# Copying the strided queries of the dilated attention groups side by side before the scores read them

## The chip, the cores and the metric

The kernel runs on one core of one Trainium2 chip. A core has five engines, each with its own in-order stream of instructions: TensorE (PE in the profile, with its weight loads listed apart as PEld), VectorE (DVE), ScalarE (ACT), GpSimd (POOL) and SyncE (SP), which here issues most DMAs. They meet through semaphores. The metric is the device time of one execution in microseconds (us); the median of the runs counts.

## The reference, cut to what matters

One decoder layer over 4096 positions: an input projection, eight heads of dilated sliding-window attention, four heads of retention, gates and an output projection. The change touches the scores of the dilated attention. Every head evaluates three branches on the same q, k and v:

```python
DILATED_BRANCHES = ((128, 1), (512, 4), (2048, 16))
def dilated_branch(q, k, v, window, dilation):
    steps = window // dilation            # 128 in every branch
    ...
    qb = gather_stride(q)                 # query t, t+d, t+2d, ...
    kb = with_prev(gather_stride(k))      # block before and own block
    vb = with_prev(gather_stride(v))
    s = jnp.einsum('bhrnqd,bhrnkd->bhrnqk', qb, kb) * (Dh ** -0.5)
    ...
    p = jnp.exp(s - m)
```

A block has 128 queries that lie `dilation` positions apart, and 256 keys. With dilation 1 the queries of a block are neighbours; with dilation 4 or 16 they are every fourth or every sixteenth position.

## The kernel before

**Stages.** Phase 1 projects q, k, v and the retention inputs and stores them in DRAM. Phase 2 does the attention and, woven between its steps, the retention and one more projection (the "filler": its matmuls are named V, Rs, Rk, Ro, Rkv, Rt). Phase 3 does the gates and the output projection. Nothing outside phase 2 is touched.

**Data of a head.** The queries of a head come from DRAM as four tiles `qq[h, t, half]`: t is 0 for the rounded-to-fp32r high part and 1 for the low rest, half is 0 for positions 0 to 2047 and 1 for the others (tiles named q_00, q_10, q_01, q_11, the first digit being t). Each tile holds 128 partitions x 2048 elements of four bytes, in the natural order of positions, and is loaded by four DMAs of 256 KB (`load_q`, issued by SP on line 547). Each of the four names has one buffer. The keys `kk[h]` stand already in an order in which a block's keys come in runs of at least eight neighbours.

**Work of a head.** `head_groups` makes 24 groups ("items") a head, gi 0 to 23, each of four blocks:
- gi 0 to 3: branch 0 (dilation 1), positions of half 0
- gi 4 to 11: branch 1 (dilation 4), alternating: one group in half 0, the next in half 1
- gi 12 to 19: branch 2 (dilation 16), each group with two blocks in either half
- gi 20 to 23: branch 0, positions of half 1

**Order.** `attention` writes the order out by hand, in half-steps: half-step t computes the scores of bank t (two blocks, one PSUM bank). An item has two half-steps; a head has 48, phase 2 has 384. In half-step t the program emits:
- `qk_bank` (line 595, PE): four matmuls S, two for each block (high part, low part). The weights, which TensorE loads before a matmul, are the 128 queries; the keys stream past them. Before the change the weights are read straight from `qq` with a step of 1, 4 or 16 elements.
- `t_bank` (line 632, PE): transposes T of the probabilities of bank t-2.
- `pv_group` (line 665, PE), at even t: the products O with the values of the item two before.
- `exp_row` (line 623, ACT) for bank t-1, `row_max` (line 616, DVE) for bank t, and `t_copy`, which moves T to SBUF (on DVE for an item's first bank, line 644, on ACT for its second, line 642).

The score tiles have two buffers: S of bank t may start once the exponentials of bank t-2 are done. So the loop S, row maximum (DVE), exponential (ACT), S runs over two half-steps. The filler's matmuls are put between the half-steps by a fixed cost table that knows nothing of the weights' step; so many half-steps, so much filler.

**Loads around the change.** At gi 0 of a head the eight DMAs of half 1 of this head are put in a list, of which two leave on SP at each half-step, between stores and other loads; SP takes them in order, and one that has to wait holds those behind it. At gi 20 the eight of half 0 of the next head follow. All DMAs of SP share the core's DMA engines.

**GpSimd in phase 2** does the low parts of the filler's inputs (line 405, 833, 836), a decay product (862) and a small power (924), 263 instructions in all.

Of the kernel before, what the change touches and what calls it, by code (L numbers as in the profile page):

```python
# [9 lines left out]
F32R = mybir.dt.float32r  # L10
# [380 lines left out]
DIL = (1, 4, 16)  # L391
# [17 lines left out]
def load_k(nc, pool, dr, h, dma=None):  # L409
    dma = dma or nc.sync.dma_start  # L410
    t = pool.tile([128, S], F32R, tag="kk", name="kk2")
    for i in range(2):
        for part in range(2):
            p0 = i * 64 + part * 32
            dma(t[p0 : p0 + 32, :].bitcast(F32), dr["k"][i, part, h])
    return t
# [63 lines left out]
def load_q(nc, pool, dr, h, i, half, dma=None):  # L480
    dma = dma or nc.sync.dma_start
    t = pool.tile([128, S // 2], F32R, tag=f"q{i}{half}", name=f"q2_{i}{half}")
    for dup in range(2):
        for part in range(2):
            p0 = dup * 64 + part * 32
            dma(t[p0 : p0 + 32, :].bitcast(F32), dr["q"][i, part, h, :, half * 2048 : (half + 1) * 2048])
    return t


def phase2(tc, io, dr, right, ahead, early3, raw, M):  # L490

    nc = tc.nc
    W2, hcp, kka, qp = (ahead[n] for n in ("w2", "hcp", "kka", "qp"))
    with ExitStack() as ctx:
        def pool(name, bufs, **kw):
            return ctx.enter_context(tc.tile_pool(name=name, bufs=bufs, reuse_waits="tile", **kw))
# [8 lines left out]
        osp = pool("p2os", 3)  # L505
        pp = pool("p2p", 3)
        vp = pool("p2v", 6)
        kkb = pool("p2kb", 1)
        psS = pool("p2pS", 2, space=PSUM)
        psT = pool("p2pT", 2, space=PSUM)  # L510
# [26 lines left out]
        def later(n, fn, *args):  # L537

            delayed.setdefault(clock[0] + n, []).append((fn, args))

        def issue_due():
            for fn, args in delayed.pop(clock[0], []):
                fn(*args)
            room = 250
            while pending and room > 0:
                dst, src = pending.pop(0)
                nc.sync.dma_start(dst, src)
                room -= dst.shape[0] * dst.shape[1] // 512
# [7 lines left out]
        qq = ahead["qq"]  # L556
# [14 lines left out]
        def need_v(h, br, g, ahead=2):  # L571

            i = vqueue.index((h, br, g))
            while vpos[0] <= min(i + ahead, len(vqueue) - 1):
                load_v(*vqueue[vpos[0]])
                vpos[0] += 1

        def qk_bank(it, bank):
            it["P", bank] = pp.tile([128, 2, 256], F32, tag="P", name="P2")
            h, br, blocks = it["h"], it["br"], it["blocks"]  # L580
            s = psS.tile([128, 512], F32, tag="S", name="S2")
            kt_ = kk[h]
            d = DIL[br]
            for j in range(2):
                i = 2 * bank + j
                r, n = blocks[i]
                half, off = divmod(n * 128 * d, 2048)
                off += r
                ks = max(n - 1, 0)
                if br == 0:  # L590
                    rhs = kt_[:, 128 * ks : 128 * ks + 256]
                else:
                    rhs = kt_.rearrange("p (m q) -> p m q", q=8 * d)[:, 16 * ks : 16 * ks + 32, 8 * r : 8 * r + 8]
                for t in range(2):
                    nc.tensor.matmul(  # L595
                        s[:, j * 256 : (j + 1) * 256],
                        qq[h, t, half][:, off : off + 127 * d + 1 : d],
                        rhs,
                        start=(j == 0 and t == 0),
                        stop=(j == 1 and t == 1),  # L600
                        skip_group_check=True,
                    )
            it["S", bank] = s
# [16 lines left out]
        def exp_row(it, i):  # L620
            nm, den = stats[it["h"]]
            sv, c0, col = s_view(it, i)
            nc.scalar.activation(  # L623
                it["P", i // 2][:, i % 2, c0:256], sv, AF.Exp, bias=nm[:, col : col + 1], scale=-1.0, accum_out=den[:, col : col + 1]
            )

        def t_bank(it, bank):

            first = 1 if it["blocks"][2 * bank][1] == 0 else 0
            t = psT.tile([128, 512], F32, tag="T", name="T2")  # L630
            for j in range(first, 4):
                nc.tensor.transpose(  # L632
                    t[:, j * 128 : (j + 1) * 128], it["P", bank][:, j // 2, j % 2 * 128 : j % 2 * 128 + 128], ident
                )
            it["T", bank] = t, first
            return 4 - first

        def t_copy(it, bank):
            t, first = it["T", bank]
            pt = it["pt"][:, 4 * bank + first : 4 * bank + 4, :].rearrange("p a b -> p (a b)")  # L640
            if bank:
                nc.scalar.activation(pt, t[:, first * 128 :], AF.Copy)  # L642
            else:
                nc.vector.tensor_copy(pt, t[:, first * 128 :])
# [8 lines left out]
        def pv_group(it):  # L653

            h, br = it["h"], it["br"]
            o = psO.tile([128, 512], F32, tag="O", name="O2")
            ops = [pv_ops(it, bank) for bank in range(2)]
            for x in range(-max(map(len, ops)), 0):
                for bank in range(2):
                    if -x > len(ops[bank]):  # L660
                        continue
                    r, n, a, m, c0 = ops[bank][x]
                    idx = r * NB_OF[br] + n
                    need_v(h, br, idx // 8)
                    nc.tensor.matmul(  # L665
                        o[64 * bank : 64 * bank + 64, c0 : c0 + 128 * m],
                        vt[h, br, idx // 8][:, idx % 8, :],
                        it["pt"][:, a : a + m, :].rearrange("p a b -> p (a b)"),
                        start=-x == len(ops[bank]),
                        stop=x == -1,  # L670
                        skip_group_check=True,
                    )
            it["O"] = o
# [63 lines left out]
        for h in range(H):  # L737
            for gi, (br, blocks) in enumerate(groups):
                it = dict(h=h, br=br, blocks=blocks, gi=gi)
# [3 lines left out]
        def pv_cost(it):  # L743
            return 190 + 218 * (4 if it["blocks"][2][1] else 3)

        def attention():


            nh = 2 * len(items)

            def half(t):
                return (items[t // 2], t % 2) if 0 <= t < nh else (None, 0)

            for t in range(nh + 12):
                cost = 0
                clock[0] = t
                issue_due()
                it, b = half(t)
                i1, b1 = half(t - 1)
                i2, b2 = half(t - 2)  # L760
                g = (t - 4) // 2 if t % 2 == 0 else -1
                gp = (t - 5) // 2 if t % 2 else -1
                if it and b == 0:
                    h, gi = it["h"], it["gi"]
                    if gi == 0:
                        stats[h] = (
                            sp.tile([128, 96], F32, tag="nm", name="nm2"),
                            sp.tile([128, 96], F32, tag="den", name="den2"),
                        )
                    if h + 1 < H:  # L770
                        if gi == 6:
                            kk[h + 1] = load_k(nc, kkb if h % 2 == 0 else kka, dr, h + 1, soon)
                        if gi == len(groups) - 4:
                            for i in range(2):
                                qq[h + 1, i, 0] = load_q(nc, qp, dr, h + 1, i, 0, soon)
                    if gi == 0:
                        for i in range(2):
                            qq[h, i, 1] = load_q(nc, qp, dr, h, i, 1, soon)
                if it:
                    qk_bank(it, b)  # L780
                    cost += 436
                if i2:
                    cost += t_bank(i2, b2) * TRN
                if 0 <= g < len(items):
                    pv_group(items[g])
                    cost += pv_cost(items[g])
                if 0 <= gp < len(items):
                    o_copy(items[gp])
                if i1:
                    exp_row(i1, 2 * b1)  # L790
                    exp_row(i1, 2 * b1 + 1)
                if i2 and b2:
                    t_copy(i2, b2)
                if it:
                    row_max(it, 2 * b)
                    row_max(it, 2 * b + 1)
                if i2 and not b2:
                    t_copy(i2, b2)
                if i1 and b1 == 1 and i1["gi"] == len(groups) - 1:
                    later(2, end_head, i1["h"])  # L800
                    cost += 2 * TRN
                yield cost
# [197 lines left out]
        n = 2 * len(items)  # L1000
# [360 lines left out]
```

## Time and profile before

| | us |
|---|---|
| median of 3 runs | 2518.52 (2517.79 to 2518.9) |
| the profiled execution: its own time | 2520.2 |
| the profiled execution: span of its trace | 2518.4 |
| of it phase 1, about | 783 |
| of it phase 2, about | 974 |
| of it phase 3, about | 761 |

The granted TensorE clock was 0.984 over the span. In the profile, a row of the windows view gives a stretch, its length, and the busy time of each engine in it with the number of instructions in brackets; a row of the timeline gives start, length, engine, source line, operation, the tile written and the tiles read, and in square brackets how long the engine had been idle and what ended that. A busy time is a union of intervals: TensorE's matmuls overlap their successors a little, since they are pipelined.

### The profile page before, as it was taken

How to read it: one execution, taken by the hardware profiler on the slowest of the kernel's cores; microseconds unless marked ns; L12 is line 12 of the kernel's file. 1: busy time of each engine (PE TensorE's matmuls, PEld its weight loads, DVE VectorE, ACT ScalarE, POOL GpSimd, SP SyncE). 2: the span in 40 equal slices, each digit the busy share in tenths (PEclk: the TensorE clock that was granted, in tenths of full speed). 3: DMA queues.
4: the chain of work that ended last, by engine and by line, in shares of the span. 5: the costliest groups of instructions: out<-in, count | busy, mean ns of one | idle time of the engine just before them, and what ended most of it. 6: DMA issues, size and time to landing. Idle time of an engine off the chain costs nothing.

```text
span 2518.4 us, 41352 instructions
## 1 busy us (share of the span) xinstructions
PE 2434.4 (97%) x14568; PEld 2085.2 (83%) x14568; DVE 1402.4 (56%) x3729; ACT 995.3 (40%) x2868; POOL 558.2 (22%) x569
## 2 busy tenths in 40 slices
PE   7999999999995999999999999998899999999998
PEld 5788888888884888888888888886789899999997
DVE  5544353354252566656666666765756556565564
ACT  4312212222123565656566656666323223232231
POOL 5312112112102222222222222223421212112110
PEclk9999999999997999999999999999899999999999
DMA  5343334334357474738374747545677565665663
GB/s 184 127 145 130 117 128 149 109 134 137 110 154 197 115 177 108 185 93 192 99 183 106 174 120 157 135 114 156 186 157 153 156 149 159 158 154 159 146 154 91
DMA packets 404063, 362.55 MB, mean 144 GB/s; under 512 B 191784, under 2 KB 334760, under 8 KB 398736
## 3 DMA queue, kind: packets, MB, share of 16 engines
q1 hardware_dynamic: 389216, 332.91, 50.6%
q10 hardware_dynamic: 14112, 25.43, 3.2%
q8 instruction: 115, 1.88, 0.3%
q0 software_dynamic: 528, 1.58, 0.2%
q14 instruction: 92, 0.75, 0.1%
HBM read 241.18 MB, written 118.64 MB: 143 GB/s over the span
## 4 chain that ended last, share of the span: by engine, by line
PE 85%; DMA 6%; DVE 3%; issue 1%; ACT 1%; POOL 1%; SPq 1%; ACTq 0%; POOLq 0%; DVEq 0%
PE S L595 12%; PE mm L49 8%; PE mm L50 8%; PE mm L51 8%; PE O L665 7%; PE T L632 6%; PE po L50 4%; PE po L51 4%; PE po L49 4%; PE g L50 4%; PE g L49 4%; PE g L51 4%; PE V L49 3%; PE V L51 2%; PE V L50 2%; DMA wb<-dr_w 1%
## 5 line engine op out<-in xcount | busy, mean ns | idle before, releaser
L616 DVE CUSTOM_DVE_ANT_0 S<-S,mask 128x256 f32<-128x256 f32 (+1 forms) x768 | 309.2, 403 | 345.5 <-PE S L595 251.0
L595 PE MATMUL S<-kk,q 128*128 128x256 f32 x1536 | 369.2, 363 | 35.3 <-DMA q<-dr_q 28.8
L595 PEld LDWEIGHTS S<-kk,q 128*128 128x128 f32 x1536 | 326.4, 274 | 68.8 <-issue 50.6
L623 ACT ACTIVATE P<-S,nm 128x256 f32<-128x256 f32 (+1 forms) x768 | 337.0, 449 | 41.8 <-DVE nm L616 21.1
L51 PE MATMUL g<-h,wg 128*128 128x256 f32 x1024 | 291.1, 284 | 0.0
L632 PE MATMUL T<-ident,P 128*128 128x128 f32 x1368 | 212.8, 273 | 0.5 <-ACT P L623 0.5
L50 PE MATMUL po<-wo,m 128*128 128x512 f32 x512 | 201.7, 394 | 0.0
L51 PEld LDWEIGHTS g<-h,wg 128*128 128x128 f32 x1024 | 198.0, 193 | 0.1
L665 PE MATMUL O<-pt,v 128*64 128x128 f32 (+1 forms) x1968 | 195.4, 324 | 0.2 <-ACT pt L642 0.2
L405 POOL TENSOR_TENSOR hc<-hr,hc 128x512 fp32r<-128x512 f32 x64 | 83.1, 1299 | 488.9 <-ACT hc L404 317.7
L49 PE MATMUL po<-wohi,m 128*128 128x512 f32 x448 | 175.3, 391 | 1.2 <-DVE x L1147 1.2
L51 PE MATMUL po<-wohi,m 128*128 128x512 f32 x448 | 176.4, 394 | 0.0
L665 PEld LDWEIGHTS O<-pt,v 128*64 128x64 f32 x1968 | 121.0, 136 | 60.4 <-issue 31.9
L632 PEld LDWEIGHTS T<-ident,P 128*128 128x128 f32 x1368 | 158.7, 141 | 1.1 <-ACT P L623 1.1
L623 ACT ACTIVATION_READ_ACCUMULATOR P<-S,nm 128x1 f32 x768 | 158.0, 206 | 0.0
L49 PE MATMUL g<-h,wg1hi 128*128 128x256 f32 x512 | 146.3, 287 | 12.0 <-ACT h L439 12.0
L41 ACT ACTIVATE m<-e 128x256 fp32r<-128x256 f32 x128 | 53.3, 417 | 256.1 <-DVE e L1100 147.1
L50 PE MATMUL g<-h,wg1hi 128*128 128x256 f32 x512 | 148.5, 290 | 2.3 <-DVE h L440 1.7
L49 PE MATMUL g<-h,wg0hi 128*128 128x256 f32 x512 | 145.5, 284 | 4.6 <-ACT e L1093 4.6
L159 POOL TENSOR_TENSOR sq<-sq,sq 128x512 f32<-128x512 f32 x56 | 76.2, 1362 | 331.4 <-ACT sq L155 331.4
L50 PE MATMUL g<-h,wg0hi 128*128 128x256 f32 x512 | 145.3, 284 | 0.0
L1154 POOL TENSOR_TENSOR rs<-v,mhalf 128x1 f32<-128x1 f32 x32 | 17.4, 544 | 555.2 <-DVE v L1152 555.2
(201 smaller groups left out, 5675.9 us busy)
## 6 DMA issues: line engine op xcount, KB each, us to landing
hr<-in_xT_dram SPq DMA_DIRECT2D x64, 512.0 KB
q<-dr_q SPq DMA_DIRECT2D x128, 256.0 KB
wb<-dr_w SPq DMA_DIRECT2D x128, 192.0 KB
o<-dr_o SPq DMA_DIRECT2D x192, 128.0 KB
v<-dr_v SPq DMA_DIRECT2D x94, 256.0 KB
xt<-in_xT_dram SPq DMA_DIRECT2D x64, 256.0 KB
dr_q<-hl SPq DMA_DIRECT2D x32, 512.0 KB
dr_k<-hl SPq DMA_DIRECT2D x32, 512.0 KB
```

Source lines behind the costliest of these rows:

```text
L41: nc.scalar.activation(dst[:, 0], src, AF.Copy)
L49: nc.tensor.matmul(out, wh, xh, start=first and i == 0, stop=False)
L50: nc.tensor.matmul(out, wh, xl, start=False, stop=False)
L51: nc.tensor.matmul(out, wl, xh, start=False, stop=last and i == n - 1)
L159: nc.gpsimd.tensor_tensor(sums[b], sums[b], sq, ALU.add)
L405: nc.gpsimd.tensor_tensor(hc[:, :, 1, :], src, hc[:, :, 0, :].bitcast(F32), ALU.subtract)
L595: nc.tensor.matmul(s[:, j * 256 : (j + 1) * 256], qq[h, t, half][:, off : off + 127 * d + 1 : d], rhs, start=(j == 0 and t == 0), stop=(j ...
L616: nc.vector.tensor_tensor_reduce(sv, sv, mask[:, it["br"], c0:256], 1.0, BIG, ALU.add, ALU.min, accum_out=nm[:, col : col + 1])
L623: nc.scalar.activation(it["P", i // 2][:, i % 2, c0:256], sv, AF.Exp, bias=nm[:, col : col + 1], scale=-1.0, accum_out=den[:, col : col + 1])
L632: nc.tensor.transpose(t[:, j * 128 : (j + 1) * 128], it["P", bank][:, j // 2, j % 2 * 128 : j % 2 * 128 + 128], ident)
L665: nc.tensor.matmul(o[64 * bank : 64 * bank + 64, c0 : c0 + 128 * m], vt[h, br, idx // 8][:, idx % 8, :], it["pt"][:, a : a + m, :].rearran ...
L1154: nc.gpsimd.tensor_tensor(rs, v, mhalf, ALU.pow)
```

## The change

A new pool of three tiles [128, 2, 4, 128] (4 KB a partition each, 12 KB in all) takes copies of the queries of an item, high and low part, block by block, 128 neighbours each. `gather_q` is called at the first half-step of an item for the item two later (`half(t + 4)`), ahead of `qk_bank`; it does nothing for dilation 1. The low part (part 1) is copied by VectorE and the high part (part 0) by GpSimd: for dilation 4 one instruction each of 128x512, for dilation 16 two each of 128x256, one for each half. `qk_bank` reads dilation 1 from `qq` as before and the others from the copies.

```diff
@@ -505,6 +505,7 @@
         vp = pool("p2v", 6)
+        qcp = pool("p2qc", 3)
         kkb = pool("p2kb", 1)
@@ -574,6 +575,25 @@
+        def gather_q(it):
+
+            h, br, blocks = it["h"], it["br"], it["blocks"]
+            if br == 0:
+                return
+            t = it["q"] = qcp.tile([128, 2, 4, 128], F32R, tag="qc", name="qc2")
+            d = DIL[br]
+            for part in range(2):
+                if br == 1:
+                    (r, n) = blocks[0]
+                    half, off = divmod(n * 128 * d, 2048)
+                    src = qq[h, part, half].rearrange("p (m r) -> p r m", r=4)[:, r, off // 4 : off // 4 + 512]
+                    (nc.vector if part else nc.gpsimd).tensor_copy(t[:, part].rearrange("p b j -> p (b j)"), src)
+                else:
+                    r = blocks[0][0]
+                    for n in range(2):
+                        src = qq[h, part, n].rearrange("p (m r) -> p r m", r=16)[:, r : r + 5 : 4, :]
+                        (nc.vector if part else nc.gpsimd).tensor_copy(t[:, part, n : n + 3 : 2, :], src)
@@ -594,7 +614,7 @@
                     nc.tensor.matmul(
                         s[:, j * 256 : (j + 1) * 256],
-                        qq[h, t, half][:, off : off + 127 * d + 1 : d],
+                        qq[h, t, half][:, off : off + 128] if br == 0 else it["q"][:, t, i, :],
                         rhs,
@@ -776,6 +796,9 @@
+                soon_it, sb = half(t + 4)
+                if soon_it and sb == 0:
+                    gather_q(soon_it)
                 if it:
                     qk_bank(it, b)
```

In the changed kernel's line numbers the copies are L591 (dilation 4) and L596 (dilation 16), the row maximum is L636, the copy of T is L664; the numbers behind the names are those of the buffers.

VectorE in the second head, from the row maxima of gi 2's second bank to those of gi 3's first bank (the row maxima are the rows "ISA", two for each block). Before:

```order
L616 ISA S_6996,nm_6839<-S_6996,mask_5372 128x256
L616 ISA nm_6839 128x1
L616 ISA S_6996,nm_6839<-S_6996,mask_5372 128x256
L616 ISA nm_6839 128x1
L927 TENSOR_SCALAR on_6823<-Ro_6671,mv_6821,rs_6822 128x128 x4
L616 ISA S_7033,nm_6839<-S_7033,mask_5372 128x256
L616 ISA nm_6839 128x1
```

The same place in the changed kernel:

```order
L636 ISA S_7066,nm_6906<-S_7066,mask_5375 128x256
L636 ISA nm_6906 128x1
L636 ISA S_7066,nm_6906<-S_7066,mask_5375 128x256
L636 ISA nm_6906 128x1
L950 TENSOR_SCALAR on_6890<-Ro_6738,mv_6888,rs_6889 128x128 x4
L591 COPY qc_7102<-q_11_6909 128x512
L636 ISA S_7106,nm_6906<-S_7106,mask_5375 128x256
L636 ISA nm_6906 128x1
```

One copy now stands between the row maxima of two banks, in every second half-step of the items gi 2 to 17. This one serves gi 5 and reads q_11, the low part of half 1, whose load was put on SP's list at gi 0 of the same head.

GpSimd in the first head, in the dilation-16 groups, between two of its hc subtractions (405) of the filler. Before:

```order
L405 TENSOR_TENSOR hc_6347<-hr_6287,hc_6347 128x4x128
L833 TENSOR_TENSOR rkl_6426<-rk_6340,rkh_6425 128x256
L836 TENSOR_TENSOR qbd_5388<-rq_6338,qbd_5387 64x2x128 x2
L405 TENSOR_TENSOR hc_6516<-hr_6287,hc_6516 128x4x128
```

The same place in the changed kernel (L856 and L859 are the old 833 and 836):

```order
L405 TENSOR_TENSOR hc_6404<-hr_6339,hc_6404 128x4x128
L596 COPY qc_6410<-q_00_5142 128x2x128
L596 COPY qc_6410<-q_01_5427 128x2x128
L596 COPY qc_6467<-q_00_5142 128x2x128
L596 COPY qc_6467<-q_01_5427 128x2x128
L856 TENSOR_TENSOR rkl_6493<-rk_6397,rkh_6492 128x256
L859 TENSOR_TENSOR qbd_5391<-rq_6395,qbd_5390 64x2x128 x2
L405 TENSOR_TENSOR hc_6583<-hr_6339,hc_6583 128x4x128
```

Two items' copies, four instructions, now stand ahead of the subtraction rkl, which a later filler matmul needs.

## The prediction

> **What bounds the kernel now.** I read the busy times by stage first (phase 1, phase 2, phase 3):
>
> ```profile
> core 0: us, PE busy (x) PEld busy (x) DVE busy (x) ACT busy (x) POOL busy (x), PEclk, DMA share, GB/s
> 0.00:783.30 783.30, 740.01 (x3161) 595.90 (x3161) 343.83 (x468) 183.12 (x275) 172.44 (x142) 0.97 0.43 139
> 783.30:1757.00 973.70, 961.51 (x6799) 827.00 (x6799) 616.88 (x2381) 607.30 (x2071) 240.56 (x263) 1.00 0.59 142
> 1757.00:2518.40 761.40, 732.84 (x4608) 662.33 (x4608) 441.66 (x880) 204.89 (x522) 145.15 (x164) 0.98 0.61 152
> ```
>
> In phase 2 TensorE is idle for only 12 of 974 us; VectorE and ScalarE stand at 62 to 63%, GpSimd at 25%. A busy TensorE need not be at its peak, so the next question is what it is busy with, and who it waits for there. The chain of work that ended last, and TensorE's waits inside phase 2 (columns: total us, times, longest):
>
> ```profile
> PE S L595 12%; PE mm L49 8%; PE mm L50 8%; PE mm L51 8%; PE O L665 7%; PE T L632 6%; PE po L50 4%; PE po L51 4%; PE po L49 4%; PE g L50 4%; PE g L49 4%; PE g L51 4%; PE V L49 3%; PE V L51 2%; PE V L50 2%; DMA wb<-dr_w 1%
> ...
> PE S L595 <- ACT P L623: 6.5, 9, 1.7
> ```
>
> The score matmuls are the largest single item of the chain, and they wait 6.5 us in all for the exponentials. So a shorter S shortens phase 2, as long as the loop through VectorE and ScalarE keeps its slack.
>
> How long is S in each dilation? One bank of dilation 1, then one of dilation 4, with the transposes that follow:
>
> ```profile
> 800.88 0.53 PEld L595 LDWEIGHTS S<-kk,q 128*128 128x128 f32 x4 [0.17 <-issue]
> 800.89 0.73 PE L595 MATMUL S<-kk,q 128*128 128x256 f32 x4
> 801.46 0.60 PE L632 MATMUL T<-ident,P 128*128 128x128 f32 x4
> ...
> 1209.31 1.02 PEld L595 LDWEIGHTS S<-kk,q 128*128 128x128 f32 x4 [0.17 <-issue]
> 1209.31 1.21 PE L595 MATMUL S<-kk,q 128*128 128x256 f32 x4
> 1210.37 0.60 PE L632 MATMUL T<-ident,P 128*128 128x128 f32 x4
> ...
> L595 PEld LDWEIGHTS S<-kk,q x1536: 186/308/337, 783.3 to 1750.8; 128*128 128x128 f32 x192
> ```
>
> Equal matmuls, but TensorE goes on to T after 0.57 us in the one and 1.06 us in the other. The weight loads (shortest/median/longest, ns) run from 186 to 337, and four of them cover 0.53 and 1.02 us: with strided queries the loads follow each other without a break and set the pace.
>
> The same over all banks, by stretches of the heads: the sums for S alone over the sixteen stretches of dilation 1, the eight of dilation 4 and the eight of dilation 16, each with 128 banks; behind the last two, the sums of all engines in the same stretches.
>
> ```profile
> sum 295.54, PE 89.97 PEld 71.88; mean PE 5.62 PEld 4.49
> sum 340.64, PE 143.37 PEld 130.01; mean PE 17.92 PEld 16.25
> sum 340.64, PE 340.64 PEld 297.99 DVE 203.16 ACT 208.36 POOL 69.75; mean PE 42.58 PEld 37.25 DVE 25.39 ACT 26.05 POOL 8.72
> sum 333.85, PE 135.81 PEld 124.51; mean PE 16.98 PEld 15.56
> sum 333.85, PE 333.61 PEld 288.46 DVE 208.74 ACT 194.65 POOL 98.23; mean PE 41.70 PEld 36.06 DVE 26.09 ACT 24.33 POOL 12.28
> ```
>
> S of one bank: 89.97 / 128 = 0.703 us (dilation 1), 143.37 / 128 = 1.120 us (4), 135.81 / 128 = 1.061 us (16). In the strided stretches TensorE is busy all the time; an item (64 in each) takes 5.32 and 5.22 us, of which VectorE works 203.16 / 64 = 3.17 and 208.74 / 64 = 3.26 us.
>
> **What it takes away.** With the queries side by side, a weight load is that of dilation 1. I take S at 0.703 us: 128 x (1.120 - 0.703) = 53.4 us and 128 x (1.061 - 0.703) = 45.8 us, **99 us less on TensorE**. The keys of dilation 4 and 16 still stream in runs of eight; no row separates their own pace, which lies between dilation 1's and today's, so this term lies between 0 and 99 us. I take 99, since the strided loads overlap by only a little and leave no gap that the keys would have to fill.
>
> In a sentence of its own: the Trainium skill (SBUF — State Buffer, Door 1: The DMA port swizzle) says that reads which leave a 16-byte line each time pay a penalty, and that one can stride for free up to 4 fp32; read as "a step of 4 is free", dilation 4 would gain nothing and the sum would be 45.8 us. The rows speak against that reading: S of dilation 4 is the slowest of the three.
>
> **What it adds on VectorE.** Each of the 128 items gets one copy of 512 elements, or two of 256. No strided copy is in the trace. The nearest rows: contiguous casts, and a two-input operation whose shortest form is contiguous and longest strided.
>
> ```profile
> L813 DVE CAST qbd<-qg 128x512 fp32r<-128x512 f32 x2 | 0.9, 468 | 0.0
> L832 DVE CAST rkh<-rk 128x256 fp32r<-128x256 f32 x31 | 9.1, 294 | 1.0
> L462 DVE TENSOR_TENSOR raw<-M,raw x6: 416/583/614, 1546.7 to 1764.8; 96x256 f32<-96x256 f32 x3, 32x256 f32<-32x256 f32 x3
> ```
>
> Low end: 0.47 us an item (0.59 as two). High end: strided elements cost L462 0.2 us more for 256, so 0.4 for 512, and should the copy run at the pace of L462 (0.61 for 256), 1.2 us. I take 0.8. VectorE's work for an item becomes 4.0 to 4.1 us, while TensorE's falls to 5.32 - 0.83 = 4.49 and 5.22 - 0.72 = 4.50: VectorE at 90%, not yet the bound. Where the copy lies in the loop is seen at a bank of dilation 4:
>
> ```profile
> 1207.05 0.98 PE L595 MATMUL S<-kk,q 128*128 128x256 f32 x4
> 1208.18 0.43 DVE L616 CUSTOM_DVE_ANT_0 S<-S,mask 128x256 f32<-128x256 f32 x1 [1.38 <-PE S L595]
> 1210.52 0.21 ACT L623 ACTIVATION_READ_ACCUMULATOR P<-S,nm 128x1 f32 x1
> 1210.67 0.43 DVE L616 CUSTOM_DVE_ANT_0 S<-S,mask 128x256 f32<-128x256 f32 x1 [1.06 <-PE S L595]
> 1212.37 1.16 PE L595 MATMUL S<-kk,q 128*128 128x256 f32 x4
> ```
>
> VectorE idles 1.38 and 1.06 us before a row maximum, waiting for S; the exponentials of the bank of 1207.05 end at 1210.73, and the bank that needs their buffer starts at 1212.37, 1.64 us later. The shorter S takes some 0.4 us off either. The copy fits into the idle time of its half-step or runs over by a few tenths, and the slack of 1.2 us takes that. Only half-steps full of filler on VectorE lose: I allow **8 us** (0 to 40; the end is 0.3 us for each of 128 items). The cover is that slack: were it gone, the whole 0.8 us x 128 = 102 us would stand on the path.
>
> **What it adds on GpSimd.** The same copies of the high part; the nearest row is a two-input operation of 512 elements:
>
> ```profile
> L405 POOL TENSOR_TENSOR hc<-hr,hc 128x512 fp32r<-128x512 f32 x64 | 83.1, 1299 | 488.9 <-ACT hc L404 317.7
> ```
>
> At the row's 1.3 us (half of it and double as ends) GpSimd comes to 69.75 / 64 + 1.3 = 2.4 us of an item's 4.5; its copies are due four half-steps later, about 9 us, and the filler's rkl and hc behind them are emitted several half-steps ahead of their matmuls. I cost this at nothing; the cover is that distance.
>
> **What it moves: the wait for the queries.** Half 1 was first read at gi 5; now VectorE reads it two items, about 10 us, earlier. A copy that waits holds the row maxima behind it, and they hold ACT and S. First and last head with a clear view, the last loads of half 1 and VectorE's arrival at gi 3; then the one DMA of 256 KB whose landing the profile gives (8.4 us), and the load on the DMA engines in that stretch:
>
> ```profile
> 918.27 1.45 SPq L547 DMA_DIRECT2D q<-dr_q  x2
> 924.53 0.43 DVE L616 CUSTOM_DVE_ANT_0 S<-S,mask 128x256 f32<-128x256 f32 x1
> ...
> 1644.88 0.99 SPq L547 DMA_DIRECT2D q<-dr_q  x2
> 1646.24 0.14 DVE L616 DVE_READ_ACCUMULATOR2_ANT nm<- 128x1 f32 x1
> ...
> v<-dr_v POOLq DMA_DIRECT2D x2, 256.0 KB, 8.4
> ...
> 1632.94:1651.29 18.35, 5.54 (x32) 4.33 (x31) 1.00 0.89 199
> ```
>
> The second of the pair issues near 918.9 and 1645.5. At 199 GB/s two of 256 KB need 2.6 us; at the row of landing 8.4. So they land 2.6 to 8.4 us after issue, middle 5.5: 921.5 to 927.3 against an arrival at 924.5, and 1648.1 to 1653.9 against 1646.4. The wait is 0 to 2.8 us in the second head and 1.7 to 7.5 in the last. About 1 us of the loop's slack covers some of it, the copy behind it adds 0.8: 0 to 34 us over eight heads. I take **16 us**, 2 a head, as the middle.
>
> **Sum.** 2518.4 - 99 + 8 + 16 = 2443 us of span. The execution took 2520.2, the median is 2518.5, so the span's scale stands for the median within 2 us: **2444 us**.
>
> **The rivals.**
> - *VectorE becomes the bound.* For: 90% at my price; the high end of 1.2 us, plus waits, makes 4.7 to 4.9 us an item. Against: its idle time before S. Saved then: 128 x (5.27 - 4.8) = 60, less 16: 2475 us. Chance 0.18.
> - *The two copies block each other* (slower than before). Place: the gather of every item; VectorE, in order, waits out GpSimd's copy, 1.3 us, on top of its own 0.9 to 1.0. VectorE's item is then 3.2 + 2.2 = 5.4 us against 5.27 now: 17 us lost, and 16 for the loads: 2551 us. It decides once copy and wait exceed 2.1 us an item. For: VectorE operations beside GpSimd's do spread,
>
> ```profile
> L157 DVE TENSOR_TENSOR h<-xt,h x64: 672/891/1778, 9.1 to 664.8; 128x512 fp32r<-128x512 f32 x64
> ```
>
> from 672 to 1778 ns, about one GpSimd operation more. Against: GpSimd's copy is released when S of the bank before ends, while VectorE has two row maxima (1.06 us) to do first, so GpSimd's is nearly over. Chance 0.08. The Trainium skill (SBUF — State Buffer, Who interferes with whom) has the rule: VectorE in a two-port mode, which copies can enter, and GpSimd fully block each other; the spread of L157 agrees that something of the kind is there.
> - *The keys set the pace, not the weights*, so S stays: nothing gained, and the loads' wait either costs its 16 us (2535) or is covered: 0.04. *Only dilation 16 gains*, a step of four costing the weight loads nothing by itself (the sums above speak against it): 2518 - 46 + 24 = 2496; 0.03.
> - *Both added costs hidden*: 2419 to 2430; 0.09.
>
> My forecast, 2430 to 2460, keeps 0.58.
>
> **How the numbers follow.** 2420 to 2500 takes in the forecast, the bound by VectorE, dilation 16 alone and most of the case of no cost: about 0.86. Faster by over 0.2% (about what a measurement of this kernel can tell from no change; 5 us): 0.58 + 0.18 + 0.03 + 0.09 = 0.88. Slower: 0.08 and half of 0.04, 0.10; within: 0.02.
>
> **What would show it.** Right: strided S at about 0.70 us a bank and weight loads near 190 ns in all; phase 2 near 899 us, phases 1 and 3 as before; one VectorE wait for q a head at gi 3. Wrong: S of 1 us; copies over 1.2 us; a VectorE copy that starts when GpSimd's ends, or is as long; TensorE waiting tens of us for L623's successor in the strided stretches.

## The result, and the profile after

| us | before | after |
|---|---|---|
| median | 2518.15 (4 runs, 2517.22 to 2518.9) | 2449.26 (4 runs, 2448.44 to 2451.97) |
| profiled execution: its own time | 2520.2 | 2448.65 |
| span of its trace | 2518.4 | 2446.9 |
| granted TensorE clock | 0.984 | 0.986 |

Ratio 0.9728, 95% interval 0.9712 to 0.9745: 69 us faster by the medians, 71.5 by the spans. Line numbers behind the new function are higher now: S is line 615 (was 595), the row maximum 636 (616), the exponential 643 (623), qbd on GpSimd 859 (836); the copies are lines 591 (dilation 4) and 596 (dilation 16).

First the windows view of the three phases, as it was shown of before (length, then busy time and instructions of PE, PEld, DVE, ACT, POOL, then clock, DMA share, GB/s):

```profile
0.00:778.35 778.35, 736.52 (x3161) 593.76 (x3161) 343.98 (x468) 183.13 (x275) 172.07 (x142) 0.98 0.43 139
778.35:1682.00 903.65, 873.90 (x6799) 730.24 (x6799) 707.53 (x2573) 602.87 (x2071) 402.30 (x455) 0.99 0.64 153
1682.00:2446.90 764.90, 733.12 (x4608) 661.88 (x4608) 433.73 (x880) 203.56 (x523) 139.91 (x165) 0.98 0.62 151
```

Phase 2, cut so that it holds the same 6799 matmuls as in the row of before, is 903.65 us long, 70.05 less than the 973.70 of before; the change is there. VectorE has 192 instructions more in it and GpSimd 192: the copies. TensorE now idles 903.65 - 873.90 = 29.75 us (12.2 before). Phase 1 is 4.95 us shorter and phase 3 3.5 longer, though no instruction of theirs changed. These parts moved by a few us between all the runs below (the start of phase 2 from 778.4 to 783.8, the part behind the last score matmul from 764.3 to 771), whichever kernel it was: a few us in a span say nothing by themselves, so stretches of phase 2 are compared instead.

How long are weight loads and matmuls of S now? The line's view gives shortest/median/longest in ns, of copies (qc) and of dilation 1 (q):

```profile
L615 PEld LDWEIGHTS S<-kk,qc x1024: 186/188/333, 804.2 to 1658.5; 128*128 128x128 f32 x171
L615 PE MATMUL S<-kk,qc x1024: 272/297/551, 804.4 to 1658.6; 128*128 128x256 f32 x171
L615 PEld LDWEIGHTS S<-kk,q x512: 186/188/338, 778.4 to 1675.9; 128*128 128x128 f32 x171
```

A load from the copies has the same median as one of dilation 1, 188 ns; over all dilations it was 308 before.

Now the same stretches as in the prediction, summed over the eight heads. The first two rows are S alone in the stretches of dilation 4 and 16, the other three all engines in gi 0 to 3, in dilation 4 and in dilation 16:

```profile
sum 291.80, PE 89.70; mean PE 11.21
sum 299.37, PE 96.84; mean PE 12.11
...
sum 162.74, PE 146.50 PEld 122.30 DVE 106.31 ACT 91.26 POOL 52.98; mean PE 18.31 PEld 15.29 DVE 13.29 ACT 11.41 POOL 6.62
sum 291.80, PE 288.74 PEld 242.33 DVE 242.95 ACT 205.69 POOL 147.24; mean PE 36.09 PEld 30.29 DVE 30.37 ACT 25.71 POOL 18.40
sum 299.37, PE 295.23 PEld 246.55 DVE 249.24 ACT 195.13 POOL 159.16; mean PE 36.90 PEld 30.82 DVE 31.16 ACT 24.39 POOL 19.90
```

and gi 0 to 3 of before, which the prediction did not show:

```profile
sum 149.35, PE 143.72 PEld 121.50 DVE 96.17 ACT 93.77 POOL 29.56; mean PE 17.96 PEld 15.19 DVE 12.02 ACT 11.72 POOL 3.69
```

From these rows comes the whole account, in us:

| | predicted | measured | from |
|---|---|---|---|
| S of dilation 4 | -53.4 | -53.7 | 143.37 to 89.70 |
| S of dilation 16 | -45.8 | -39.0 | 135.81 to 96.84 |
| the stretches of dilation 4 and 16 shrink by less | +8 | +9.3 | (53.7 - 48.8) + (39.0 - 34.5) |
| gi 0 to 3 get longer | +16 | +13.4 | 149.35 to 162.74 |
| gi 20 to 23, start of phase 2, part behind | 0 | -1.6 | -0.1 - 5.0 + 3.5 |
| span | -75 | -71.5 | |

S of dilation 4 takes 89.70 / 128 = 0.701 us a bank, as predicted; S of dilation 16 stays at 96.84 / 128 = 0.757. TensorE's waits (total, times, longest) are few but three times as long as the 6.5 us of before:

```profile
PE S L615 <- ACT P L643: 18.5, 20, 2.4
PE S L615 <- POOL qc L596: 1.8, 1, 1.8
```

Where gi 0 to 3 lose is seen in the timeline at gi 3 of the last head:

```profile
1577.24 0.72 PE L615 MATMUL S<-kk,q 128*128 128x256 f32 x4
1579.77 0.72 PE L615 MATMUL S<-kk,q 128*128 128x256 f32 x4
...
1582.07 0.62 DVE L591 CAST qc<-q 128x512 fp32r<-128x512 f32 x1 [4.75 <-DMA raw<-dr_st]
1582.61 0.42 DVE L636 CUSTOM_DVE_ANT_0 S<-S,mask 128x256 f32<-128x256 f32 x1
1583.71 0.47 ACT L643 ACTIVATE P<-S,nm 128x256 f32<-128x256 f32 x1 [2.79 <-DVE nm L636]
1584.88 1.19 PE L615 MATMUL S<-kk,qc 128*128 128x256 f32 x4 [2.37 <-ACT P L643]
```

VectorE stands for 4.75 us before a copy. The row maxima of the bank of 1577.24 lie behind it; the exponential waits 2.79 us for them, and the bank of 1584.88, which needs their buffer, waits 2.37 us for the exponential. In each of the heads 2 to 8 VectorE stands once like this, for 1.5 to 4.75 us, 20 us in all, and these seven stretches are 12.0 us longer than before. In the first head it stands for 0.3 us only; that stretch is 1.4 us longer at a granted clock of 0.79 (0.83 before). The releaser is given as the load of another tile; that it is the queries' is not said by this row, and is tested below (late5).

### The profile page after: what moved, and what is told of

The parts are those of the page before. It is cut to its first block, busy times and chain, and to the rows that moved or that the text cites. A ratio compares the mean times of both kernels' runs of the same rounds, so it can differ in the third digit from the quotient of the medians.

```text
span 2446.9 us, 41800 instructions
## 1 busy us (share of the span) xinstructions
PE 2343.5 (96%) x14568; PEld 1985.9 (81%) x14568; DVE 1485.2 (61%) x3921; ACT 989.6 (40%) x2868; POOL 714.3 (29%) x761
## 4 chain that ended last, share of the span: by engine, by line
PE 74%; DMA 10%; DVE 5%; issue 2%; ACT 2%; POOL 2%; SPq 1%; ACTq 0%; POOLq 0%; DVEq 0%
PE S L615 8%; PE mm L49 8%; PE mm L50 8%; PE mm L51 8%; PE O L685 6%; PE T L652 5%; PE po L49 3%; PE po L50 3%; PE po L51 3%; PE g L50 3%; PE g L49 3%; PE g L51 3%; PE V L49 3%; DMA wb<-dr_w 2%; PE V L51 2%; PE V L50 2%
## 5 line engine op out<-in xcount | busy, mean ns | idle before, releaser
L636 DVE CUSTOM_DVE_ANT_0 S<-S,mask 128x256 f32<-128x256 f32 (+1 forms) x768 | 308.5, 402 | 168.7 <-PE S L615 139.1
L615 PE MATMUL S<-kk,qc 128*128 128x256 f32 x1024 | 186.5, 306 | 17.1 <-ACT P L643 11.8
L615 PEld LDWEIGHTS S<-kk,qc 128*128 128x128 f32 x1024 | 149.8, 190 | 45.5 <-issue 28.9
L652 PEld LDWEIGHTS T<-ident,P 128*128 128x128 f32 x1368 | 163.7, 141 | 1.1 <-ACT P L643 1.1
```

The source lines that it names most:

```text
L615: nc.tensor.matmul(s[:, j * 256 : (j + 1) * 256], qq[h, t, half][:, off : off + 128] if br == 0 else it["q"][:, t, i, :], rhs, start=(j == ...
L636: nc.vector.tensor_tensor_reduce(sv, sv, mask[:, it["br"], c0:256], 1.0, BIG, ALU.add, ALU.min, accum_out=nm[:, col : col + 1])
L652: nc.tensor.transpose(t[:, j * 128 : (j + 1) * 128], it["P", bank][:, j // 2, j % 2 * 128 : j % 2 * 128 + 128], ident)
```

## The experiments

Theory: (1) the step of the weights is the pace of S in both dilations; (2) the loss in gi 0 to 3 is the early read of half 1; (3) the loss in the strided stretches is VectorE's added work; (4) dilation 16 keeps 0.757 because of its keys. Rivals: only one dilation gains; S becomes shorter for another reason than the copies; the losses come from GpSimd, or from S being too short for the loop. Each diff is against the changed kernel. The first four ran beside a median of before of 2519.66 us, the others beside 2517.8.

**Only dilation 4, only dilation 16.**

```diff
-            if br == 0:
+            if br != 1:     # only16: br != 2
...
-    qq[h, t, half][:, off : off + 128] if br == 0 else it["q"][:, t, i, :],
+    it["q"][:, t, i, :] if br == 1 else qq[h, t, half][:, off : off + 127 * d + 1 : d],     # only16: br == 2
```

> Copies for dilation 4 alone; dilation 16 reads its queries with a step of 16 again. Theory (weight loads with a step set the pace of S in both dilations; the first copy of half 1 waits for its loads): S of dilation 4 falls to 0.70 us a bank, S of dilation 16 stays at 1.06; 54 us less on TensorE, 13 us lost at gi 3, 5 us in the loop: about 2480 us. Rival (a step of four elements costs weight loads nothing by itself): S of dilation 4 stays near 1.1 and the time is 2518 to 2535 us.

> Copies for dilation 16 alone; the first copy of a head now comes at gi 10, long after the loads of half 1. Theory: S of dilation 16 at 0.76 us a bank, 39 us less, 4 to 5 us lost in the loop, no wait for loads: about 2484 us, and the stretch gi 0 to 3 as before. Rival (the stretch gi 0 to 3 is longer because of the copies' work on VectorE or the new pool, not because of the loads): those stretches stay 13 us longer in all, 2497 us.

Measured: only4 2483.47 us, ratio 0.9857 (0.9841 to 0.9874); only16 2486.11, ratio 0.9872 (0.9858 to 0.9887). S alone by the windows view, dilation 4 and 16 in only4, then dilation 16 in only16, and all engines in gi 0 to 3 of only16:

```profile
sum 293.68, PE 90.69; mean PE 11.34
sum 333.83, PE 135.82; mean PE 16.98
...
sum 300.97, PE 96.86; mean PE 12.11
...
sum 150.28, PE 143.59 PEld 121.35 DVE 96.30 ACT 93.87 POOL 29.55; mean PE 17.95 PEld 15.17 DVE 12.04 ACT 11.73 POOL 3.69
```

In only4, S of dilation 4 falls to 0.709 us a bank and S of dilation 16 stays where it was (135.82, before 135.81); in only16 dilation 16 alone falls, to 0.757. Each dilation's gain comes from its own copies, and both gain. And gi 0 to 3 lose only where dilation 4 is copied (150.28 us here, 161.80 in only4). This is where the reads of half 1 were moved; the copies of gi 12 and later read tiles that have long been there.

**The copies are made but not read.**

```diff
-    qq[h, t, half][:, off : off + 128] if br == 0 else it["q"][:, t, i, :],
+    qq[h, t, half][:, off : off + 127 * d + 1 : d],
```

> All copies are made, but all scores read the queries with their step, as before the change: the cost of the copies without their gain. Theory: S as before, the slack in the loop is back and hides the copies' work; what stays is the wait for half 1's loads, 13 us in the stretches gi 0 to 3: about 2531 us (5 less if the earlier start of phase 2 belongs to the new pool). Rival (the copies cost VectorE and GpSimd time on the path everywhere): 10 to 30 us more than that, spread over the strided stretches.

Measured: 2538.1 us, ratio 1.0077 (1.0062 to 1.0092). The copies alone cost 18.4 us, some 7 more than expected. S alone in dilation 4 and 16, then all engines in gi 0 to 3, dilation 4 and dilation 16:

```profile
sum 344.13, PE 144.30; mean PE 18.04
sum 337.88, PE 136.19; mean PE 17.02
...
sum 161.75, PE 146.58 PEld 122.26 DVE 104.35 ACT 90.64 POOL 53.51; mean PE 18.32 PEld 15.28 DVE 13.04 ACT 11.33 POOL 6.69
sum 344.13, PE 343.92 PEld 299.93 DVE 242.21 ACT 210.68 POOL 147.27; mean PE 42.99 PEld 37.49 DVE 30.28 ACT 26.34 POOL 18.41
sum 337.88, PE 335.51 PEld 289.41 DVE 251.02 ACT 195.91 POOL 158.49; mean PE 41.94 PEld 36.18 DVE 31.38 ACT 24.49 POOL 19.81
```

S is as strided and as slow as before (143.37 and 135.81 us there), so the shorter S comes from reading the copies and from nothing else. Two costs stay: 161.75 - 149.35 = 12.4 us in gi 0 to 3, and (344.13 - 340.64) + (337.88 - 333.85) = 7.5 us in the strided stretches. The expectation had the second at nothing, since with the long S the slack was to hide the copies. In the first six heads it does (0.4 us in all); 7.1 of the 7.5 us lie in the last two.

And there little of it is waiting. TensorE idles for (344.13 - 343.92) + (337.88 - 335.51) = 2.6 us of the strided stretches, against 0.2 before. For the other 5.2 us it is busy longer with the same matmuls, and its granted clock (third number from the end of a row) accounts for most of that. Dilation 4 of the seventh head, before and in this run; then three stretches of this run, TensorE alone:

```profile
1530.52:1572.80 42.28, 42.28 (x294) 36.94 (x294) 28.84 (x104) 26.56 (x90) 10.97 (x11) 1.00 0.64 144
1539.16:1583.22 44.06, 44.03 (x293) 37.81 (x293) 33.72 (x112) 26.20 (x88) 20.72 (x21) 0.96 0.59 137
...
1539.70:1543.10 3.40, 3.40 (x20) 0.50 0.73 195
1666.00:1669.40 3.40, 3.40 (x20) 0.50 0.76 192
1741.10:1744.50 3.40, 3.40 (x17) 0.50 0.98 256
```

Before, the clock stood at 1.00 through all strided stretches; here it fell to half three times in the last two heads. Half the clock for 10.2 us is a loss of about 5.1 us (an estimate from these rows), nearly all of the 5.2. Each time TensorE had waited for an exponential until less than 1 us earlier (3.7, 1.8 and 1.2 us), but a wait of 1.8 us in the changed kernel (seventh head, dilation 16) had no such stretch behind it, so what decides isn't shown. In the changed kernel the shares are other: of its 9.3 us, 7.0 are idle time of TensorE (3.06 + 4.14 us idle, 0.24 before), and one stretch of 3.4 us at half the clock lies in dilation 4 of the last head, right behind the wait of the timeline above.

**Half 1 read one item later.** The copies of gi 5, the first that need half 1, are emitted a whole item later; all others as they were.

```diff
-                if soon_it and sb == 0:
+                if soon_it and sb == 0 and soon_it["gi"] != 5:
                     gather_q(soon_it)
+                next_it, sb = half(t + 2)
+                if next_it and sb == 0 and next_it["gi"] == 5:
+                    gather_q(next_it)
```

> Only the gather for gi 5, the first that reads half 1, is moved: from the first half-step of gi 3 to the first of gi 4. Theory (its loads land about then): the 13 us of the stretches gi 0 to 3 fall to 0 to 4, 2437 to 2440 us. Rival (the stretch is longer because VectorE has more to do there): no change, 2449 us, or a loss of the same size at gi 4.

Measured: 2434.72 us, ratio 0.9667 (0.9652 to 0.9681). Gi 0 to 3:

```profile
sum 150.51, PE 144.90 PEld 122.49 DVE 102.09 ACT 93.73 POOL 48.80; mean PE 18.11 PEld 15.31 DVE 12.76 ACT 11.72 POOL 6.10
```

The stretch is back at 150.5 (149.35 before, 162.74 after), and the strided stretches are unchanged (290.8 and 299.4). One item more for the loads, and the wait is gone: the loss was the wait for the queries' landing, not the copies themselves.

**Neighbouring keys for dilation 16.** The score matmuls of dilation 16 stream 256 neighbouring keys where they took runs of eight.

```diff
-                if br == 0:
+                if br != 1:
```

> As the changed kernel, but the scores of dilation 16 stream 256 neighbouring keys instead of runs of eight (the scores of dilation 16 are then of other keys). Theory (the 0.06 us a bank by which dilation 16 stays above 0.70 is the pace of its keys): S of dilation 16 falls from 0.757 to about 0.70 us a bank and its stretches from 299 to 292 to 296 us. Rival (it is the weights, read from the copies): S of dilation 16 stays at 0.757.

Measured: 2447.97 us (one run). S of dilation 16:

```profile
sum 291.22, PE 87.62; mean PE 10.95
```

87.62 / 128 = 0.685 us a bank instead of 0.757, and the stretch is 8.2 us shorter (299.37 to 291.22). So the copied queries leave a bank of dilation 16 at the pace of its keys. Dilation 4, whose keys come in runs of eight too, does not show it (0.701). In the program its runs lie 32 elements apart, those of dilation 16 lie 128 apart; whether this distance makes the difference wasn't tried. The whole time is only 1.3 us shorter than after's, since other stretches of this run were longer (gi 0 to 3 165.3, dilation 4 294.5); with one run, the stretch is the measure.

**All copies on GpSimd, all copies on VectorE.**

```diff
-   (nc.vector if part else nc.gpsimd).tensor_copy(...)
+   nc.gpsimd.tensor_copy(...)     # alldve: nc.vector
```

> GpSimd makes both copies of an item, VectorE none. Theory (the loop's loss of 9 us in the strided stretches is VectorE's extra work, and VectorE is what the late loads hold up): GpSimd has 3.6 to 4.0 of an item's 4.5 us and still keeps up; strided stretches 585 instead of 591 us, stretches gi 0 to 3 at 150 instead of 163: about 2430 us. Rival (GpSimd becomes the bound and holds the filler's inputs): strided stretches longer than 591 us, TensorE waiting for GpSimd's tiles, 2450 us or more.

> VectorE makes both copies, GpSimd none. Theory (each VectorE copy is 0.61 us, or 0.27 twice, when GpSimd leaves it alone, so two parts cost VectorE 1.2 us an item where one part now costs 0.76 to 1.08 with GpSimd beside it): VectorE at 4.4 of 4.5 us an item, the loop loses 5 to 20 us more than now: 2454 to 2470 us. Rival (the two engines' blocking of each other is what the loop loses): single copies shorter and the strided stretches no longer than now, 2440 to 2450 us.

Measured: allpool 2428.04 us (2425.82 to 2429.36), ratio 0.9641 (0.9625 to 0.9657); alldve 2479.3, ratio 0.9844 (0.9829 to 0.9859). Gi 0 to 3, dilation 4 and dilation 16 of allpool, then dilation 4 and dilation 16 of alldve:

```profile
sum 150.40, PE 143.72 PEld 121.48 DVE 96.20 ACT 93.57 POOL 63.97; mean PE 17.96 PEld 15.19 DVE 12.02 ACT 11.70 POOL 8.00
sum 287.36, PE 286.89 PEld 241.44 DVE 203.46 ACT 203.81 POOL 207.84; mean PE 35.86 PEld 30.18 DVE 25.43 ACT 25.48 POOL 25.98
sum 298.03, PE 295.71 PEld 247.93 DVE 207.69 ACT 193.13 POOL 211.92; mean PE 36.96 PEld 30.99 DVE 25.96 ACT 24.14 POOL 26.49
...
sum 306.05, PE 293.35 PEld 242.59 DVE 281.40 ACT 204.52 POOL 87.22; mean PE 36.67 PEld 30.32 DVE 35.17 ACT 25.56 POOL 10.90
sum 318.79, PE 303.33 PEld 247.81 DVE 286.83 ACT 200.22 POOL 107.50; mean PE 37.92 PEld 30.98 DVE 35.85 ACT 25.03 POOL 13.44
```

In allpool both costs go at once. The strided stretches take 585.4 us (after: 591.2), 5.8 of the 9.3 us that they had lost; 3.5 stay without any copy on VectorE. Most of them lie in dilation 16 of the last head (38.44 us, after: 37.44): by the trace TensorE waits 1.83 us there for VectorE, which itself waits 1.74 us for a store (`dr_ret<-on`), and 3.4 us at a granted clock of 0.50 follow. No run tests this. GpSimd is busy for 72% of dilation 4 (207.84 of 287.36) and holds nobody up. And gi 0 to 3 are back at 150.4, although the reads of half 1 stand as early in the program as in the change. The view of line 591 of allpool shows where the wait went, and the timeline its longest piece, in the second head:

```profile
L591 POOL CAST qc<-q x128: 1084/1134/1532, 796.6 to 1593.6; 128x512 fp32r<-128x512 f32 x128
...
  DMA q<-dr_q: 13.7, 4
...
911.55 1.13 POOL L591 CAST qc<-q 128x512 fp32r<-128x512 f32 x1 [8.09 <-DMA q<-dr_q]
```

GpSimd now stands for the loads, four times, 13.7 us in all, and this costs next to nothing: with the 8.09 us in it, gi 0 to 3 of the second head take 17.41 us, as before. (In the heads 3 to 7 GpSimd, with two copies to make, arrives later and waits 0.7 us at most.) The work behind its copy is due half-steps later, while behind VectorE's copy stood the next row maximum. The wait itself was not the loss; the queue it stood in was.

In alldve VectorE works 281.40 of 306.05 us (92%) in dilation 4 and 286.83 of 318.79 (90%) in dilation 16, and TensorE waits 37.1 us for the exponentials. The strided stretches are 33.6 us longer than after's (624.8 against 591.2), more than the 5 to 20 us expected; 21.0 of them are idle time of TensorE. This is the prediction's first rival, reached by doubling VectorE's share.

**VectorE's copy a half-step later than GpSimd's.** This is meant to keep the two copies of an item apart (`gather_q` is given the parts to copy; that piece of the edit is left out here):

```diff
-                    gather_q(soon_it)
+                    gather_q(soon_it, (0,))
+                soon_it, sb = half(t + 3)
+                if soon_it and sb == 0:
+                    gather_q(soon_it, (1,))
```

> GpSimd's copy as now, VectorE's copy of the same item one half-step later, when GpSimd's is over. Theory (the two block each other where they meet): VectorE's copies fall from means of 756 and 538 ns towards their shortest, 610 and 280; strided stretches 585 us instead of 591; the wait at gi 3 gets 2.3 us shorter a head, 8 to 12 us in all: 2433 to 2440 us. Rival (the spread of the copies has another cause): the means stay, and only the wait at gi 3 shrinks, 2440 us.

Measured: 2434.42 us, ratio 0.9668 (0.9653 to 0.9682). The copies of dilation 4, after and apart (line's view, shortest/median/longest in ns):

```profile
L591 DVE CAST qc<-q x64: 607/636/1587, 795.5 to 1608.0; 128x512 fp32r<-128x512 f32 x64
L591 POOL CAST qc<-q x64: 1092/1120/1630, 795.8 to 1609.9; 128x512 fp32r<-128x512 f32 x64
```

```profile
L593 DVE CAST qc<-q x64: 606/646/1590, 801.6 to 1600.5; 128x512 fp32r<-128x512 f32 x64
```

This one missed, and the edit did not do what it was meant to. VectorE's copies start 2.1 to 2.2 us behind GpSimd's of the same item in the median (0.8 and 0.0 in the changed kernel), but 25 of its 64 copies of dilation 4 and 52 of its 128 of dilation 16 still run beside some copy of GpSimd (after: 18 and 35). One of them, with nothing of GpSimd beside it but the second copy of the first row:

```profile
1349.73 2.20 POOL L593 CAST qc<-q 128x512 fp32r<-128x512 f32 x2
1350.90 1.55 DVE L593 CAST qc<-q 128x512 fp32r<-128x512 f32 x1
```

VectorE's copies of dilation 16 lost their longest stalls (939 ns at most, 1474 after; means 502 and 538), but those of dilation 4 are as long as they were (means 780 and 756), and the strided stretches fall by 1.8 us only (290.9 + 298.5 against 591.2). So the run leaves open what the meeting of the two copies costs. The gain of the kernel comes from gi 0 to 3 (148.3 us): VectorE's read of half 1 was moved by a half-step too, and that was enough for the loads.

## Why the prediction was right, point by point

- **The pace of S is the weights' step, in both dilations.** Right in mechanism: loads of 188 ns, and only4 and only16 gain each for itself. The Trainium skill's sentence on striding up to 4 fp32 (SBUF — State Buffer, Door 1: The DMA port swizzle), read as "a step of 4 is free", falls for weight loads: only4 takes 36 us off. The rival that went with it (2496) falls too.
- **The size of that term: 99 predicted, 92.6 measured.** The step that was off is "I take 99, since the strided loads overlap by only a little and leave no gap that the keys would have to fill". It held for dilation 4 (53.7 against 53.4) and not for dilation 16 (39.0 against 45.8), whose keys stream at 0.757 us a bank; with neighbouring keys it is 0.685. The bound of 0 to 99 had named this, and the value was taken at its end.
- **VectorE's copies: 0.8 us an item assumed.** In phase 2 VectorE's busy time grew by 707.53 - 616.88 = 90.65 us, 0.71 for each of 128 items. The loss in the loop, 8 predicted, was 9.3, and its place was named ("half-steps full of filler"): 8.3 us of it lie in the last two heads, 5.0 of these in the seventh, where VectorE is fullest. In dilation 4 the seventh head takes 39.05 us with VectorE busy for 35.17, the head before it 35.70 with 30.62 (windows view, same columns as above):

```profile
1357.18:1392.88 35.70, 35.48 (x293) 30.04 (x294) 30.62 (x110) 26.10 (x90) 18.59 (x22) 1.00 0.71 165
1467.35:1506.40 39.05, 36.65 (x293) 29.84 (x293) 35.17 (x114) 26.05 (x88) 20.67 (x21) 1.00 0.66 153
```

  Of the strided stretches only the seventh head's hold the lines 458 to 474 on VectorE, single instructions of up to 1.7 us. With the copies on GpSimd that stretch of the seventh head is 36.36 us. "The slack of 1.2 us takes that" holds elsewhere: with the slack of before, unread loses 0.4 us in six heads. What no term of the sum held is the lower clock behind some waits, about 5 us in unread and less in the changed kernel.
- **GpSimd's copies at nothing.** Right: its busy time in phase 2 grew by 402.30 - 240.56 = 161.7 us, 1.26 for each item (1.3 assumed), and allpool, with twice that work there, is the fastest of all. The one wait of TensorE that the profile gives to a GpSimd copy (1.8 us, seventh head) cost nothing of its own: the exponentials that the same bank needs ended 0.02 us before that copy.
- **The wait for half 1 of the queries: 16 predicted, 13.4 measured.** Right in place and size; 12.0 us of it lie in the seven heads that show the wait. late5 takes it away by time, allpool by moving it to another queue. The last head's wait, 4.75 us by the timeline above, lies inside the 1.7 to 7.5 that it was priced at.
- **The rivals.** VectorE as the bound (2475) is real, but one copy away: alldve, at 2479.3. Both costs hidden (2419 to 2430) is what allpool reached. The blocking of the two engines (2551) exists, as the last section shows, at a fraction of its price: in the changed kernel the seven VectorE copies of dilation 4 that meet a GpSimd copy and nothing else of GpSimd take 1.09 us in the mean, those that meet nothing 0.63.

Phase 2 came out at 903.65 us instead of some 899, and the sum of the whole span held within 4 us because the terms' errors stand on both sides: 6.6 us too much gain, 2.6 too much wait, 1.3 too little loss, and 1.6 from parts that the change doesn't touch. That they cancel so nearly is luck; the mechanisms of the three large terms are not.

## What to carry to other kernels

Weights that TensorE loads with a step between elements can set the pace of short matmuls: compare the time from one matmul to the next operation for equal shapes and different steps, and price a copy on an idle engine against it. Put such a copy on the engine whose queue holds nothing that is due soon, not on the one whose single copy is shortest: here GpSimd needs 1.12 us and VectorE 0.64, and all copies on GpSimd win over the shared ones, with 0.9641 (0.9625 to 0.9657) of the time of before against 0.9728 (0.9712 to 0.9745). When an added read comes earlier than the first read of before, ask when its load lands, and what stands behind the waiting instruction.

## What the runs showed of the hardware

**A strided copy on VectorE is cheap, unless GpSimd works beside it.** The copies of dilation 16 on VectorE take 0.39 us in the median for 256 elements that lie 16 apart, but up to 1.47 (after); those of dilation 4 up to 1.59 (shown above). It need not be GpSimd's own copies, though they do it too (the pair shown with apart): alldve has none there, and its longest is longer still. The line's view of alldve, with GpSimd's line 859, and the same line (836) of before:

```profile
L591 DVE CAST qc<-q x128: 610/634/1757, 798.2 to 1641.3; 128x512 fp32r<-128x512 f32 x128
...
L859 POOL TENSOR_TENSOR qbd<-rq,qbd x64: 715/762/1142, 770.2 to 1677.2; 64x256 fp32r<-64x256 f32 x64
```

```profile
L836 POOL TENSOR_TENSOR qbd<-rq,qbd x64: 716/725/736, 771.7 to 1716.3; 64x256 fp32r<-64x256 f32 x64
```

Two places in the timeline of alldve, two copies each (the second row of each pair is GpSimd's filler):

```profile
816.85 1.92 DVE L591 CAST qc<-q 128x512 fp32r<-128x512 f32 x2
817.14 2.23 POOL L859 TENSOR_TENSOR qbd<-rq,qbd 64x256 fp32r<-64x256 f32 x2
...
1403.29 2.28 DVE L591 CAST qc<-q 128x512 fp32r<-128x512 f32 x2
1403.41 1.66 POOL L405 TENSOR_TENSOR hc<-hr,hc 128x512 fp32r<-128x512 f32 x1 [9.37 <-ACT hc L404]
```

Undisturbed, two copies take some 1.2 us; beside GpSimd's two operations they take 1.92, and these take 2.23 instead of 1.45. Both sides are stretched. Of the 128 copies of dilation 4 in alldve, none of the 83 that no GpSimd instruction overlaps takes more than 654 ns; the others, 45, take up to 1757. The row maximum (line 636) isn't stretched: 279/432/444 ns after, 269/432/465 before. The Trainium skill has such a rule (SBUF — State Buffer, Who interferes with whom): copies of VectorE that may use two ports and GpSimd block each other. These rows agree with it for the copies; whether a strided copy uses two ports no run shows.

**Keys in runs of eight** cost nothing in dilation 4 (0.701 us a bank, dilation 1 0.703 in the trace of before) and 0.07 us in dilation 16 (0.757 against 0.685 with neighbouring keys). Why the one and not the other stays open.
